# Wider weight blocks and equal token groups in the HGRN2 mixer of a two-layer diffusion backbone

## The chip, the cores and the metric

The kernel runs on one core of a Trainium2 chip. Its metric is the device time of one execution in microseconds (us); the median of three runs before the change is 1749.47 us, from 1747.55 to 1752.41. Names of engines in the profile: PE is TensorE's matrix product, PEld its loading of the stationary operand, DVE is VectorE, ACT is ScalarE, POOL is GpSimd, SP is SyncE, which here issues the large loads.

## The reference

Two layers on 768 tokens of width 1024: 512 latent tokens and a prefix of 256 context tokens, which reads only itself. Each layer is a mixer and a SwiGLU feed-forward network (FFN, inner width 2816). Each sub-layer has an RMS norm and a modulation (shift, scale) ahead of it, and a norm and a gate behind it. Shift, scale and gate are products of two conditioning vectors with `mod_w` (1024 x 6144 per layer). Layer 0 mixes by gated linear attention and grouped-query attention. Layer 1, where most of the change lies, mixes by HGRN2:

```python
fq, f_fwd, f_bwd, fi, fog = _split(h @ w_in, ODD_SIZES)          # five parts of 1024 columns
q = _heads(jax.nn.silu(fq), HGRN_HEADS)                           # 8 heads of 128
i = _heads(fi, HGRN_HEADS)                                        # the values
og = _heads(fog, HGRN_HEADS)                                      # the gates
for d, f in enumerate((f_fwd, f_bwd)):
    log_f = logaddexp(log(lb[d]), log1p(-lb[d]) + log_sigmoid(f)) # forget gates
    k = -expm1(log_f)
    dirs.append(_directional_scan(q, k, i, log_f, n_ctx, reverse=(d == 1)))
o_lat = _gated_readout(dirs[0][1] + dirs[1][1], og[:, :, n_ctx:], out_norm)   # rms(o) * silu(og)
```

The readout goes through `odd_w_out`, and then the last FFN follows. All is fp32.

## The kernel before

An fp32 product is made of three products of the kind fp32r: each operand is split into a high part (H, rounded) and a rest (L), and `mm3` (line 706) issues high by high, high by low and low by high into one accumulation in PSUM. All matmuls are recorded at line 371 and all transposes by PE at line 374. The contraction over 1024 has 8 k-tiles of 128, so a product of one 128-wide stationary tile has 24 matmuls.

**Weights** come in units of 128 x 1024 elements (512 KB). `unit` (from line 685) loads one on SP into a `raw` buffer (three of them), ACT casts it to the high part `wH` (line 699), and DVE subtracts it for the low part `wL` (line 700); there are four pairs `wH`/`wL`. `nat_units` cuts half the k-tiles of a block of columns into units: one of 4 k-tiles by 256 columns, or two of 2 k-tiles by 512.

**Two forms of product.** `gemm_T` keeps the weights stationary and moves tokens, in groups of up to 512 columns of a PSUM tile of two banks with 512 columns each; its result has features on the partitions. It makes the queries, the forget gates (`ff`, two directions for 8 heads, 768 tokens each, so 16 products) and the queries and keys of the first mixer (`gqk`, four products). `gemm_nat` keeps a tile of 128 tokens stationary and moves the weights; its result has tokens on the partitions (`nat`). It makes the values (6 token tiles, as three pairs) and the gates (4 latent tiles, as two pairs), in blocks of 256 columns.

**The order in time around the change.** (1) Near the end of FFN 0, `values()` in `run` makes the first 512 columns of the values, in pieces between the norms of token tiles that come out of the FFN; some units go to tiles that the FFN no longer uses (`go`, `uo`, `macc`). These are the rows `nat<-oH`, `nat<-ogo` and the like. (2) `odd_mixer` makes the other 512 columns, and a generator `late` beside it loads 24 pieces of `mod_w` (tiles `mraw`, three buffers, on SP at line 477), which DVE sums (lines 552 and 554, `macc`). PE adds the sums across partitions (`mod_acc`), DVE copies them (`modrows`, line 485), and PE transposes them (`modT`). (3) For 8 heads, `prep` makes forget gates and queries and `head` scans; pieces of three heads are interleaved by hand with `go`, each call of which advances generators to their next `yield`. (4) Behind the last head come the `gate` blocks, between the last scans: a Silu on ACT (line 1443, into a tile of the tag `mraw` with two buffers) and a product on DVE with the readout. (5) `gated_T` transposes the gated readout (`catT`, ACT copies it at line 1270 and DVE makes its low part), and `out_proj` multiplies by `odd_w_out` (`oproj`), whose units pass through the same `raw` buffers.

Each engine works through its own queue in order, and so does each DMA queue. The queues' order is settled when the program is built. While `self.pinned` is set (heads and gates), PE keeps the order in which the code issues its work; the weight casts and splits on ACT and DVE may come to stand elsewhere than where the code has them.

Of the kernel before, what the change touches and what calls it, by code (L numbers as in the profile page):

```python
# [17 lines left out]
P = 128  # L18
# [321 lines left out]
class Net:  # L340
# [384 lines left out]
    def nat_units(self, w, c0, n, half, to=None):  # L725
        src = w[half * 512 : half * 512 + 512, c0 : c0 + n].rearrange("(k p) m -> p k m", p=P)
        if 4 * n <= WU:
            return [self.unit(src, 4, n, to=to)]
        return [self.unit(src[:, 2 * q : 2 * q + 2, :], 2, n) for q in range(2)]

    def gemm_nat(self, w, c0, n, h, tiles, evac, psum=None, us=None):

        us = us or self.nat_units(w, c0, n, 0) + self.nat_units(w, c0, n, 1)
        kp = KD // len(us)
        for t0 in tiles:
            pt = (psum or self.mm_tile)("nat").rearrange("p (a b) -> p a b", a=2)
# [12 lines left out]

# [308 lines left out]
    def even_mixer(self, h, mix, zu, last):  # L1058
# [7 lines left out]
        groups = ((0, 512), (512, 256))  # L1066
# [56 lines left out]
        def qk(c):  # L1123
            Ws = {x: self.unit_cols(w, x * P) for x in (c, c + 2)}
            yield
            for x in (c, c + 2):
                pt = self.mm_tile(f"gqk{x}")
                for g in groups:
                    self.gemm_T(pt, Ws[x], h, (g,))
                    if g is groups[-1]:  # L1130
                        t = gqk[x // 2] if c == 0 else mixg.tile([P, NT], F32, tag=f"gqk{x // 2}", bufs=1, name=f"gqk{x}")
                        if x < 2:
                            nc.scalar.mul(t, pt[:, :NT], 0.125)
                            gq[c] = t
                        else:
                            nc.scalar.copy(t, pt[:, :NT])
                            gk[c] = t
                    yield
# [186 lines left out]
    def odd_values(self, fi, h, c0, tiles, us=None):  # L1325


        def ev(t0, pt):
            self.nc.scalar.copy(fi[:, t0 : t0 + 2, c0 : c0 + 256], pt[:, :, :256])  # L1329

        self.gemm_nat(self.I["odd_w_in"][0], 3 * D + c0, 256, h, tiles, ev, us=us)

    def odd_mixer(self, h, fi):
# [14 lines left out]
        with self.pool("hg") as gp:  # L1348
            ones = gp.tile([P, CTX], F32, tag="ones", name="ones")
            nc.gpsimd.memset(ones, 1.0)  # L1350
            def prep(hd, given):
# [5 lines left out]
                for d in range(2):  # L1357
                    pt = self.mm_tile(f"ff{hd}{d}")
                    W = self.unit_cols(w, (1 + d) * D + hd * P)
                    self.gemm_T(pt, W, h, ((512, 256),))  # L1360
                    yield
                    self.gemm_T(pt, W, h, ((0, 512),))
                    sg = gp.tile([P, NT], F32, tag="sg", bufs=2, name="sg")
                    nc.scalar.activation(sg, pt[:, :NT], AF.Sigmoid)
# [73 lines left out]
            def gate(c0):  # L1438
                us = self.nat_units(w, 4 * D + c0, 256, 0) + self.nat_units(w, 4 * D + c0, 256, 1)

                def eo(t0, pt):
                    s = self.wp.tile([P, WU], F32, tag="mraw", bufs=2, name="silu")[:, :512].rearrange("p (a n) -> p a n", a=2)
                    nc.scalar.activation(s, pt[:, :, :256], AF.Silu)
                    o = fi[:, t0 : t0 + 2, c0 : c0 + 256]
# [24 lines left out]
            g = [gate(c0) for c0 in (0, 256, 512, 768)]  # L1469
            go(scan, g[0])  # L1470
            go(outs, old)
            go(g[0])
            go(outs, old, scan)
            go(g[1], g[1])
            go(scan, scan)
            go(g[2])
            go(scan)
            go(g[2])
            go(scan)
            go(g[3], g[3])  # L1480
# [152 lines left out]
    def run(self):  # L1633
# [132 lines left out]
        def ending(ys):  # L1766
            ep = self.open_pool("e0b")

            def values():

                to = [[fp.tile([P, D], F32R, tag=x, bufs=1, name=f"o{x}") for x in ("go", "uo")]]
# [3 lines left out]
                self.odd_values(ys, h1, 0, (4,), us)  # L1775
                yield
                self.odd_values(ys, h1, 0, (0,), us)
                yield
                us2 = [u for half in range(2) for u in self.nat_units(I["odd_w_in"][0], 3 * D + 256, 256, half)]
                self.odd_values(ys, h1, 256, (4,), us2)  # L1780
                yield
                self.odd_values(ys, h1, 0, (2,), us)
                self.odd_values(ys, h1, 256, (0, 2), us2)
# [80 lines left out]
```

## Time and profile before

| What | Time |
|---|---|
| median of three runs | 1749.47 us (1747.55 to 1752.41) |
| the profiled execution | 1749.34 us |
| its span (first to last instruction) | 1747.5 us, so 1.84 us lie around it |
| mean granted clock of TensorE | 0.993 of full speed |
| ending of FFN 0 with the first values | 930 to 980 us of the span |
| second half of the values | 980 to 1027 us |
| heads, with the forget gates | 1027 to 1267 us |
| gates, and start of the output projection | 1267 to 1350 us |

A row of the timeline has the start in the span, the duration, engine and line, output and operands, form and number of instructions, and, in brackets, how long the engine idled before and what released it. Durations of matmuls overlap, since they are pipelined: the distance of two starts is what a matmul takes. "nat<-wH,x" is a product of the high weights with a token tile x; `wL` is the low part. SPq is SP's DMA queue. A row of groups has the number of instructions, their busy time and mean in ns, and the idle time before them with its main releaser.

### The profile page before, as it was taken

The numbers are of one execution on the slowest core, as the hardware profiler recorded it, in microseconds if no ns is written. First come the engines' busy times: TensorE is split into PE (matmuls) and PEld (weight loads), VectorE is DVE, ScalarE is ACT, GpSimd is POOL, SyncE is SP. The second block draws the span as 40 slices with busy tenths as digits, with TensorE's granted clock in tenths as the row PEclk, the third lists the DMA queues.
The fourth block names the chain that finished last, engine by engine and source line by source line (L and its number), as shares of the span: only waits on it lengthen the run. The fifth ranks groups of instructions, "written<-read, shape, count | busy, mean of one in ns | idle before, by whom it ended". The sixth has DMA issues, their size and how long they took to land. (4 is left out here: it accounts for less than half of the span.)

```text
span 1747.5 us, 32790 instructions
## 1 busy us (share of the span) xinstructions
PE 1700.9 (97%) x13732; PEld 1526.0 (87%) x13732; DVE 1280.9 (73%) x2036; ACT 857.8 (49%) x1473; POOL 74.2 (4%) x93
## 2 busy tenths in 40 slices
PE   6999999999999999999999999999999999999998
PEld 4889986788999989989998988889898899989997
DVE  5879658735966979787668658787764678878785
ACT  5545557746543333333347336666644664344342
POOL 1004100001000000000001000000000100000000
PEclk8999999999999999999999999999999999999999
DMA  8731013154322424332234752121114333233333
GB/s 318 222 112 39 3 39 107 36 156 139 113 90 73 153 77 156 109 110 61 73 123 143 262 160 63 48 62 50 50 62 133 121 98 108 86 102 106 99 106 120
DMA packets 169647, 187.23 MB, mean 107 GB/s; under 512 B 6262, under 2 KB 140956, under 8 KB 169500
## 3 DMA queue, kind: packets, MB, share of 16 engines
q1 hardware_dynamic: 167568, 181.56, 32.8%
q10 hardware_dynamic: 1932, 3.59, 0.7%
q8 instruction: 107, 1.75, 0.4%
q14 instruction: 40, 0.33, 0.1%
HBM read 175.66 MB, written 9.46 MB: 106 GB/s over the span
## 5 line engine op out<-in xcount | busy, mean ns | idle before, releaser
L371 PE MATMUL nat<-wH,x 128*128 128x256 f32 (+1 forms) x1216 | 229.0, 287 | 0.4 <-issue 0.4
L754 ACT CAST wH<-raw 128x1024 fp32r<-128x1024 f32 x120 | 124.5, 1051 | 197.2 <-PE acc L371 86.2
L700 DVE TENSOR_TENSOR wL<-raw,wH 128x1024 fp32r<-128x1024 f32 (+1 forms) x126 | 151.3, 1206 | 84.3 <-ACT wH L699 83.9
L371 PEld LDWEIGHTS nat<-wH,x 128*128 128x128 f32 x1216 | 193.3, 193 | 3.8 <-ACT y L1329 0.8
L755 DVE TENSOR_TENSOR wL<-raw,wH 128x1024 fp32r<-128x1024 f32 x120 | 145.2, 1221 | 64.9 <-ACT wH L754 64.8
L699 ACT CAST wH<-raw 128x1024 fp32r<-128x1024 f32 (+1 forms) x126 | 128.9, 1038 | 127.8 <-PE nat L371 34.4
L371 PE MATMUL nat<-wL,x 128*128 128x256 f32 (+1 forms) x608 | 173.4, 285 | 0.0
L371 PE MATMUL acc<-wH,gH 128*128 128x512 f32 x440 | 171.8, 390 | 0.0
L371 PE MATMUL acc<-wH,gL 128*128 128x512 f32 x440 | 171.5, 390 | 0.0
L371 PE MATMUL acc<-wL,gH 128*128 128x512 f32 x440 | 171.5, 390 | 0.0
L847 DVE TENSOR_TENSOR y<-y,acc 128x1024 f32<-128x1024 f32 x135 | 115.2, 863 | 37.0 <-PE acc L371 32.8
L554 DVE SCALAR_TENSOR_TENSOR macc<-mraw,scT,macc 128x1024 f32<-128x1024 f32 x98 | 122.6, 1277 | 10.7 <-DMA mraw<-in_mod_w_dram 10.4
L371 PE MATMUL ff<-x,wH 128*128 128x512 f32 (+1 forms) x512 | 127.6, 340 | 0.0
L624 POOL TENSOR_TENSOR rs<-ms,neghalf 128x1 f32<-128x1 f32 (+2 forms) x62 | 58.0, 937 | 1543.2 <-DVE ms L622 1543.1
L371 PEld LDWEIGHTS nat<-wL,x 128*128 128x128 f32 x608 | 117.3, 193 | 0.0
L371 PE MATMUL oproj<-wH,x 128*128 128x512 f32 x320 | 102.5, 397 | 3.2 <-ACT x L1270 3.2
L371 PEld LDWEIGHTS acc<-wH,gL 128*128 128x128 f32 x440 | 82.6, 188 | 17.3
L371 PEld LDWEIGHTS acc<-wH,gH 128*128 128x128 f32 x440 | 82.7, 188 | 16.6
L371 PEld LDWEIGHTS acc<-wL,gH 128*128 128x128 f32 x440 | 82.7, 188 | 16.5
L371 PEld LDWEIGHTS ff<-x,wH 128*128 128x128 f32 x512 | 87.3, 190 | 10.1
L955 ACT COPY qkh<-arr 128x512 f32<-128x512 f32 x112 | 70.1, 642 | 36.3 <-DVE arr L960 32.1
L371 PE MATMUL ff<-x,wL 128*128 128x256 f32 (+1 forms) x256 | 86.2, 337 | 0.0
(344 smaller groups left out, 4047.2 us busy)
## 6 DMA issues: line engine op xcount, KB each, us to landing
mraw<-in_mod_w_dram SPq DMA_DIRECT2D x96, 512.0 KB, 4.8
raw<-in_ffn_w_gate_dram SPq DMA_DIRECT2D x44, 512.0 KB, 3.7
raw<-in_ffn_w_up_dram SPq DMA_DIRECT2D x44, 512.0 KB, 3.8
raw<-in_ffn_w_down_dram SPq DMA_DIRECT2D x44, 512.0 KB, 3.6
raw<-in_odd_w_in_dram SPq DMA_DIRECT2D x40, 512.0 KB, 3.7
raw<-in_even_w_in_dram SPq DMA_DIRECT2D x16, 512.0 KB, 4.6
x<-xr SPq DMA_DIRECT2D x14, 512.0 KB, 2.6
xr<-x SPq DMA_DIRECT2D x14, 512.0 KB, 8.1
```

The source lines that it names most:

```text
L371: return self.pin(self.nc.tensor.matmul(*a, **k))
L554: nc.vector.scalar_tensor_tensor(a, u, w, a, op0=ALU.mult, op1=ALU.add)
L624: nc.gpsimd.tensor_tensor(rs, ms, self.neghalf.to_broadcast([P, w]), op=ALU.pow)
L699: nc.scalar.copy(H[:, :m], raw[:, :m])
L700: nc.vector.tensor_tensor(L[:, :m], raw[:, :m], H[:, :m].bitcast(F32), op=ALU.subtract)
L754: self.nc.scalar.copy(H, f)
L755: self.nc.vector.tensor_tensor(L, f, H.bitcast(F32), op=ALU.subtract)
L847: nc.vector.tensor_tensor(y, y, pt, op=ALU.add)
L955: nc.scalar.copy(qkv[:, :, :, half, :], dst)
```

## The change

It has three parts.

First, the values and the gates are made in blocks of 512 columns, each of four units of 2 k-tiles by 512, in place of blocks of 256 with two units of 4 k-tiles. In the second half of the values there is one block, with ten steps of `late` behind each of three pairs of token tiles, where there were two blocks with five. The gates are two blocks, each in four pieces of one token tile, where there were four blocks of two pieces; the product of a gate with the readout is put off to a list that `gated()` works off, and the calls of `go` stand in another order. In the ending of FFN 0 the one block is made in halves of k (`nat_part`): tokens 4 and 5 with the first half, then tiles 0 and 1, then the second halves, and so on; the first half's units lie in the FFN's old tiles, the second half's in `wH` and `wL`.

Second, products over 768 tokens go as two groups of 384, each in a bank of its own, in place of 512 and 256: the 16 `ff` products of the heads and the four `gqk` products of the first mixer. The offset given to `gemm_T` puts tokens 384 to 767 at column 512 of the PSUM tile, and ACT reads the result as 2 x 384.

Third, as a consequence, 7655 rows stand in PE's list where 8135 stood: 480 matmuls fewer. The number of loads is the same.

```diff
-        return [self.unit(src[:, 2 * q : 2 * q + 2, :], 2, n) for q in range(2)]
+        return [self.unit(src[:, 2 * q : 2 * q + 2, :], 2, n, to=to and to[q]) for q in range(2)]
...
+    def nat_part(self, pt, us, h, t, half):
+
+        kp = 4 // len(us)
+        for k in range(4):
+            W = us[k // kp]
+            self.mm3(
+                pt, h.hl(4 * half + k, slice(t * P, t * P + P)), (W[0][:, k % kp, :], W[1][:, k % kp, :]),
+                half == 0 and k == 0, half == 1 and k == 3,
+            )
...
-        groups = ((0, 512), (512, 256))
+        groups = ((0, 384, 0), (384, 384, -128))
...
-                    self.gemm_T(pt, Ws[x], h, (g,))
+                    self.gemm_T(pt, Ws[x], h, (g[:2],), g[2])
...
-        for c0 in range(512, D, 256):
-            us = self.nat_units(w, 3 * D + c0, 256, 0) + self.nat_units(w, 3 * D + c0, 256, 1)
-            for t0 in (4, 0, 2):
-                self.odd_values(fi, h, c0, (t0,), us)
-                for _ in range(5):
-                    next(late, None)
+        us = [u for half in range(2) for u in self.nat_units(w, 3 * D + 512, 512, half)]
+        for t0 in (4, 0, 2):
+            self.gemm_nat(w, 3 * D + 512, 512, h, (t0,), lambda t, pt: nc.scalar.copy(fi[:, t : t + 2, 512:D], pt), us=us)
+            for _ in range(10):
+                next(late, None)
...
-                    self.gemm_T(pt, W, h, ((512, 256),))
+                    self.gemm_T(pt, W, h, ((384, 384),), -128)
                     yield
-                    self.gemm_T(pt, W, h, ((0, 512),))
+                    self.gemm_T(pt, W, h, ((0, 384),))
...
-                us = self.nat_units(w, 4 * D + c0, 256, 0) + self.nat_units(w, 4 * D + c0, 256, 1)
...
-                for t0 in (0, 2):
-                    self.gemm_nat(w, 4 * D + c0, 256, h, (t0,), eo, us=us)
-                    yield
+                us = [u for half in range(2) for u in self.nat_units(w, 4 * D + c0, 512, half)]
+                for t in range(LT):
+                    pt = self.mm_tile("nat")[:, :512]
+                    for half in range(2):
+                        self.nat_part(pt, us[2 * half : 2 * half + 2], h, t, half)
+                    s = self.wp.tile([P, WU], F32, tag="mraw", bufs=2, name="silu")[:, :512]
+                    nc.scalar.activation(s, pt, AF.Silu)
+                    o = fi[:, t, c0 : c0 + 512]
+                    todo.append((o, s))
+                    yield
...
-            g = [gate(c0) for c0 in (0, 256, 512, 768)]
+            g = [gate(c0) for c0 in (0, 512)]
...
-                us = [u for half in range(2) for u in self.nat_units(I["odd_w_in"][0], 3 * D, 256, half, to[half])]
+                us = [self.nat_units(w, 3 * D, 512, 0, to)]
...
+                part(4, 0)
                 yield
+                us.append(self.nat_units(w, 3 * D, 512, 1))
+                part(0, 0)
                 yield
+                part(4, 1)
                 yield
+                part(0, 1)
+                part(2, 0)
+                part(2, 1)
```

The pieces move instructions on two engines whose queues PE waits for. The first place is DVE's queue where the values end and the heads begin. `macc` are the sums of `mod_w`, `gt` is a copy of gate columns, `L700` the weight splits, `modrows` the copy that PE waits for, `pr` the first work of a head. Before:

```order
L554 SCALAR_TENSOR_TENSOR macc_10238<-mraw_10304,scT,macc_10238 128x1024
L497 TENSOR_TENSOR modcol_10001<-modT,col 128x8
L497 TENSOR_TENSOR modcol_10002<-modT,col 128x8
L600 TENSOR_TENSOR gc_10229<-modcol_10001,col 128x8
L554 SCALAR_TENSOR_TENSOR macc_10238<-mraw_10357,scT,macc_10238 128x1024
L606 COPY gt_10233<-gcT_10231 8x128
L700 TENSOR_TENSOR wL<-raw,wH 128x1024 x2
L485 COPY modrows<-mod_acc 128x512
L1375 MEMSET pr 128x1
```

Now:

```order
L497 TENSOR_TENSOR modcol_9863<-modT,col 128x8
L497 TENSOR_TENSOR modcol_9864<-modT,col 128x8
L600 TENSOR_TENSOR gc_9979<-modcol_9863,col 128x8
L554 SCALAR_TENSOR_TENSOR macc_9988<-mraw_10051,scT,macc_9988 128x1024
L606 COPY gt_9983<-gcT_9981 8x128
L554 SCALAR_TENSOR_TENSOR macc_9988<-mraw_10054,scT,macc_9988 128x1024
L554 SCALAR_TENSOR_TENSOR macc_9988<-mraw_10057,scT,macc_9988 128x1024
L700 TENSOR_TENSOR wL<-raw,wH 128x1024 x3
L485 COPY modrows<-mod_acc 128x512
L1378 MEMSET pr 128x1
```

Two more of the sums stand behind the `gt` copy, and three weight splits, not two, ahead of `modrows`.

The second place is ACT's queue at the end of the gates: the last two Silus, the casts of `odd_w_out` (line 699), and the first copies of `catT`. Before:

```order
L615 DMA gv_14268<-gd_10235 128x1024
L1509 ACT_TABLE_LOAD
L699 CAST wH<-raw 128x1024
L1443 ACTIVATE silu<-nat 128x512
L699 CAST wH<-raw 128x1024 x2
L1443 ACTIVATE silu<-nat 128x512
L1270 ACTIVATE x_14194<-catT,col 128x512 x2
```

Now (lines 1443 and 1270 have become 1448 and 1281):

```order
L615 DMA gv_13776<-gd_9985 128x1024
L1524 ACT_TABLE_LOAD
L1448 ACTIVATE silu<-nat 128x512
L699 CAST wH<-raw 128x1024 x3
L1448 ACTIVATE silu<-nat 128x512
L1281 ACTIVATE x_13702<-catT,col 128x512 x2
L699 CAST wH<-raw 128x1024
```

The next to last Silu has moved ahead of the casts, and all three casts stand between the two Silus.

More of the change, by code (lines that the diff above doesn't have):

```diff
@@ L1128, in qk @@
                 for g in groups:
-                    self.gemm_T(pt, Ws[x], h, (g,))
+                    self.gemm_T(pt, Ws[x], h, (g[:2],), g[2])
                     if g is groups[-1]:
                         t = gqk[x // 2] if c == 0 else mixg.tile([P, NT], F32, tag=f"gqk{x // 2}", bufs=1, name=f"gqk{x}")
+                        pv, tv = (v.rearrange("p (b n) -> p b n", b=2)[:, :, :384] for v in (pt, t))
                         if x < 2:
-                            nc.scalar.mul(t, pt[:, :NT], 0.125)
+                            nc.scalar.mul(tv, pv, 0.125)
                             gq[c] = t
                         else:
-                            nc.scalar.copy(t, pt[:, :NT])
+                            nc.scalar.copy(tv, pv)
                             gk[c] = t
@@ L1322, in att_prep @@
                 nc.gpsimd.tensor_tensor(x, x, rs[:, hs][:, :, None].to_broadcast([P, n, 64]), op=ALU.mult)
[L1325 to L1331, printed above, removed]
     def odd_mixer(self, h, fi):
@@ L1359, in prep @@
                     W = self.unit_cols(w, (1 + d) * D + hd * P)
-                    self.gemm_T(pt, W, h, ((512, 256),))
+                    self.gemm_T(pt, W, h, ((384, 384),), -128)
                     yield
-                    self.gemm_T(pt, W, h, ((0, 512),))
+                    self.gemm_T(pt, W, h, ((0, 384),))
                     sg = gp.tile([P, NT], F32, tag="sg", bufs=2, name="sg")
-                    nc.scalar.activation(sg, pt[:, :NT], AF.Sigmoid)
+                    pv, sv = (v.rearrange("p (b n) -> p b n", b=2)[:, :, :384] for v in (pt, sg))
+                    nc.scalar.activation(sv, pv, AF.Sigmoid)
                     lb, lb1, nlb1 = (x[:, d, hd : hd + 1] for x in (self.lb, self.lb1, self.nlb1))
@@ L1438, in gate, with gated @@
             def gate(c0):
-                us = self.nat_units(w, 4 * D + c0, 256, 0) + self.nat_units(w, 4 * D + c0, 256, 1)
[L1441 to L1444, printed above, removed]
+                us = [u for half in range(2) for u in self.nat_units(w, 4 * D + c0, 512, half)]
[8 more added lines that the diff above has]
+                    yield
+            todo = []
+            def gated():
+                while todo:
+                    o, s = todo.pop(0)
                     nc.vector.tensor_tensor(o, o, s, op=ALU.mult)
-                for t0 in (0, 2):
-                    self.gemm_nat(w, 4 * D + c0, 256, h, (t0,), eo, us=us)
-                    yield
             def go(*xs):
@@ L1468, in odd_mixer @@
                 outs, old, scan = scan, new, head(hd, *given[0])
-            g = [gate(c0) for c0 in (0, 256, 512, 768)]
+            g = [gate(c0) for c0 in (0, 512)]
             go(scan, g[0])
+            gated()
             go(outs, old)
             go(g[0])
+            gated()
             go(outs, old, scan)
-            go(g[1], g[1])
+            go(g[0])
+            gated()
+            go(g[0])
+            gated()
             go(scan, scan)
-            go(g[2])
+            go(g[1])
             go(scan)
-            go(g[2])
+            go(g[1])
             go(scan)
-            go(g[3], g[3])
+            gated()
+            for _ in range(2):
+                go(g[1])
+                gated()
             self.pinned = False
@@ L1769, in values, with part @@
             def values():
+                w = I["odd_w_in"][0]
                 to = [[fp.tile([P, D], F32R, tag=x, bufs=1, name=f"o{x}") for x in ("go", "uo")]]
                 to.append([fp.tile([P, D], F32R, tag="macc", bufs=2, name=f"o{x}") for x in "HL"])
-                us = [u for half in range(2) for u in self.nat_units(I["odd_w_in"][0], 3 * D, 256, half, to[half])]
+                us = [self.nat_units(w, 3 * D, 512, 0, to)]
+                pts = {}
+                def part(t0, half):
+                    if half == 0:
+                        pts[t0] = self.mm_tile("nat").rearrange("p (a b) -> p a b", a=2)
+                    for a in range(2):
+                        self.nat_part(pts[t0][:, a, :], us[half], h1, t0 + a, half)
+                    if half:
+                        nc.scalar.copy(ys[:, t0 : t0 + 2, 0:512], pts.pop(t0))
                 yield
-                self.odd_values(ys, h1, 0, (4,), us)
+                part(4, 0)
                 yield
-                self.odd_values(ys, h1, 0, (0,), us)
+                us.append(self.nat_units(w, 3 * D, 512, 1))
+                part(0, 0)
                 yield
-                us2 = [u for half in range(2) for u in self.nat_units(I["odd_w_in"][0], 3 * D + 256, 256, half)]
-                self.odd_values(ys, h1, 256, (4,), us2)
+                part(4, 1)
                 yield
-                self.odd_values(ys, h1, 0, (2,), us)
-                self.odd_values(ys, h1, 256, (0, 2), us2)
+                part(0, 1)
+                part(2, 0)
+                part(2, 1)
                 ep.release()
```

## The prediction, made before the changed kernel ran

> **What bounds the kernel now.** The page was read first, then the busy times by stretch for the four places the change touches, then the timeline of single instructions inside them.
>
> ```profile
> span 1747.5 us, 32790 instructions
> PE 1700.9 (97%) x13732; PEld 1526.0 (87%) x13732; DVE 1280.9 (73%) x2036; ACT 857.8 (49%) x1473; POOL 74.2 (4%) x93
> ```
>
> PE is busy for 97% of the span, but that share is a mean over the stages, so the places must be looked at singly. The stretches below are, in order: the ending of the first FFN with the first half of the values (930 to 980), the second half of the values (to 1027), the heads with the ff gates (to 1267), the gates and the start of the output projection (to 1350). The columns are the length, busy time and instruction count of PE, its weight loads, DVE, ACT and POOL, the granted clock, the DMA share and GB/s.
>
> ```profile
> 930.00:980.00 50.00, 47.41 (x326) 42.88 (x325) 35.21 (x49) 38.57 (x85) 6.12 (x9) 1.00 0.52 178
> 980.00:1027.00 47.00, 46.13 (x382) 43.95 (x380) 31.26 (x30) 9.95 (x14) 0.32 (x1) 1.00 0.77 257
> 1027.00:1267.00 240.00, 239.19 (x2875) 212.10 (x2872) 181.99 (x397) 145.51 (x246) 8.46 (x6) 1.00 0.19 56
> 1267.00:1350.00 83.00, 79.39 (x796) 75.19 (x795) 47.37 (x86) 38.52 (x59) 2.02 (x2) 0.98 0.32 103
> ```
>
> PE idles 2.6, 0.9, 0.8 and 3.6 us in them, with the clock at full in all but the last (0.98). So here a product removed shortens the span, as long as weights and operands keep up. No other engine is above 77% (DVE in the third). The question is then what a product costs by its width. A duration of one matmul (0.40 us for two, 0.28 for one) overlaps its neighbour's, so the starts must be used, first and last of a steady run for each width:
>
> ```profile
> 1267.92 0.40 PE L371 MATMUL nat<-wH,x 128*128 128x256 f32 x2
> ...
> 1272.24 0.40 PE L371 MATMUL nat<-wH,x 128*128 128x256 f32 x2
> ```
>
> Between these starts stand 12 triples of 256 columns (each k-tile is one row of two and one of one): 4.32/36 = 0.1200 us each. The output projection has the same roles, tokens stationary and weights moving, at 512 columns:
>
> ```profile
> 1344.11 0.62 PE L371 MATMUL oproj<-wH,x 128*128 128x512 f32 x2
> ...
> 1352.27 0.62 PE L371 MATMUL oproj<-wH,x 128*128 128x512 f32 x2
> ```
>
> 12 triples in 8.16 us: 0.2267 us each. For 384 columns, with both kinds of stationary operand, the first mixer has a run:
>
> ```profile
> 564.61 0.51 PE L371 MATMUL E<-x,wH 128*128 128x384 f32 x2
> ...
> 567.73 0.51 PE L371 MATMUL ab<-x,dH 128*128 128x384 f32 x2
> ```
>
> 6 triples in 3.12 us: 0.1733 us. The three points lie on one line: 53.3 ns more for every 128 columns, and 13.3 ns that each matmul pays whatever its width (120.0 − 106.7).
>
> **The change part by part.**
>
> *Blocks of 512.* 960 matmuls of 256 columns become 480 of 512. Values: 4 blocks x 6 token tiles x 8 k x 3 = 576, now 288; gates: 4 x 4 x 8 x 3 = 384, now 192. Each pair costs 0.2400 now and 0.2267 then, 13.3 ns less. Where the 512-wide rows are slowest, at 1241.15 to 1241.85, three take 0.70 us, 0.2333 each, which leaves 6.7 ns a pair:
>
> ```profile
> 1241.15 0.62 PE L371 MATMUL ff<-x,wH 128*128 128x512 f32 x2
> ...
> 1241.85 0.62 PE L371 MATMUL ff<-x,wH 128*128 128x512 f32 x2
> ```
>
> That run follows small work; the long runs have 0.2267 without exception, so I take 13.3. Ending of FFN 0: 144 pairs, 1.92 us; second half of the values: 144 pairs, 1.92; gates: 192 pairs, 2.56. Together 6.4 us, at the lower bound 3.2.
>
> The Trainium skill ("TensorE: Matmul & The Clock Gate", section "Back-to-back issue gap") gives the gap of one isolated matmul as N/2.4 + 2.5 ns, so a part of 2.5 ns that does not grow with the width, where the rows have 13.3. By it the sum of the widening would be 480 x 2.5 = 1.2 us; the trace disagrees, and the sum goes by the trace.
>
> *Groups of 384.* 512 + 256 becomes 384 + 384, as many matmuls and as many columns. On the ff products the pair is in the rows:
>
> ```profile
> 1242.53 0.62 PE L371 MATMUL ff<-x,wH 128*128 128x512 f32 x2
> ...
> 1245.25 0.62 PE L371 MATMUL ff<-x,wH 128*128 128x512 f32 x2
> ...
> 1246.28 0.40 PE L371 MATMUL ff<-x,wH 128*128 128x256 f32 x2
> ...
> 1248.44 0.40 PE L371 MATMUL ff<-x,wH 128*128 128x256 f32 x2
> ```
>
> 0.680 per k at 512 and 0.360 at 256 (2.72/4 and 2.16/6), together 1.040, against 2 x 0.520 for two of 384: nothing, in the ff gates and in the first mixer alike. The first half of a head's ff product now also takes tokens that the later chain does not wait for alone (48 matmuls of 0.1733 either way); ACT's activation reads two banks in place of one piece, same 768 columns. I count 0, with ±1 us for the 20 places (16 ff products, four of the first mixer).
>
> *Weight units.* The 40 loads and splits stay 40, each with as many bytes; what changes is that a block needs four units before it ends, where two sufficed.
>
> ```profile
> raw<-in_odd_w_in_dram SPq DMA_DIRECT2D x40, 512.0 KB, 3.7
> L699 ACT CAST wH<-raw 128x1024 fp32r<-128x1024 f32 (+1 forms) x126 | 128.9, 1038 | 127.8 <-PE nat L371 34.4
> L700 DVE TENSOR_TENSOR wL<-raw,wH 128x1024 fp32r<-128x1024 f32 (+1 forms) x126 | 151.3, 1206 | 84.3 <-ACT wH L699 83.9
> ```
>
> A unit is ready 3.7 + 1.04 + 1.21 ≈ 6 us after its load starts. The split buffers are four and the raw ones three. In a block's last token tile the first buffer comes free when 18 of 24 matmuls are still ahead: 18 x 0.227 = 4.1 us before the end. Three raw units then lie loaded, so cast and split of the next first unit fit (2.25 us); only its fourth, whose load can start when the first raw is released, is 6 us away, and PE needs it 4.1 us + the scan pieces between + three units of 6 matmuls (4.1 us) later. I count 0 here. If that cover is gone, it is the rival (c) below.
>
> *Ending of FFN 0.* ACT's cast before the first late token tile already waited for a load:
>
> ```profile
> 964.97 1.05 ACT L699 CAST wH<-raw 128x1024 fp32r<-128x1024 f32 x1 [4.36 <-DMA raw<-in_odd_w_in_dram]
> ```
>
> Behind it in ACT's queue stand the hf scalings of the next token tile, which PE's products need. With products that are shorter by 1.9 us, I let 0.5 us of it be lost to this wait: −1.4, between 0 (the load sets the end) and −1.9.
>
> *From the values to the heads.* The second half of the values runs beside the modulation sums (24 loads of 512 KB) and ends at a row of sums that goes through DVE and back to PE. DVE's and PE's rows:
>
> ```profile
> 967.72 44.97 SPq L477 DMA_DIRECT2D mraw<-in_mod_w_dram  x24
> 1018.57 1.29 DVE L554 SCALAR_TENSOR_TENSOR macc<-mraw,scT,macc 128x1024 f32<-128x1024 f32 x1 [1.45 <-DMA mraw<-in_mod_w_dram]
> 1025.89 1.23 DVE L700 TENSOR_TENSOR wL<-raw,wH 128x1024 fp32r<-128x1024 f32 x1 [3.37 <-ACT wH L699]
> 1027.23 0.69 DVE L485 COPY modrows<-mod_acc 128x512 f32<-128x512 f32 x1
> 1026.09 1.06 PE L371 MATMUL mod_acc<-macc,one 128*32 128x512 f32 x8
> 1027.97 0.66 PE L374 MATMUL modT<-ident,modrows 128*128 128x128 f32 x4 [0.81 <-DVE pr L1375]
> 1028.38 0.48 PE L371 MATMUL ff<-x,wH 128*128 128x256 f32 x2
> ```
>
> The sums end at 1019.9 and PE comes to them at 1026.1: 6.2 us of slack, of which the shorter products (1.4 + 1.9) take about 3.3. So the ring of loads doesn't become the bound. On DVE three weight splits, not two, stand ahead of the modrows copy; three times 1.22 after 1019.9 is 1023.6, and PE arrives at about 1022.8 and would find modrows ready at 1024.5 at the latest, with the 0.8 us idle of today grown by up to 1. I count the whole −1.9 and let the 1 us be in the range. At worst the gain of this part and of the one before is eaten here.
>
> *End of the gates.* Here a stall goes. PE, then ACT:
>
> ```profile
> 1327.43 1.04 PE L374 MATMUL catT<-ident,y 128*128 128x128 f32 x8
> 1331.67 0.50 PE L371 MATMUL oproj<-wH,x 128*128 128x512 f32 x1 [3.21 <-ACT x L1270]
> 1326.19 1.05 ACT L699 CAST wH<-raw 128x1024 fp32r<-128x1024 f32 x1 [0.94 <-PE nat L371]
> 1329.50 1.04 ACT L699 CAST wH<-raw 128x1024 fp32r<-128x1024 f32 x1 [2.26 <-DMA raw<-in_odd_w_out_dram]
> 1330.45 0.59 ACT L1443 ACTIVATE silu<-nat 128x512 f32<-128x512 f32 x1
> 1330.94 1.26 ACT L1270 ACTIVATE x<-catT,col 128x512 fp32r<-128x512 f32 x2
> ```
>
> PE ended the last gate at 1327.4 and transposed; the copies of those transposes (L1270) stood on ACT behind the last Silu, this behind a cast, and this behind a load of the output weights until 1329.50. In the changed order ACT has three casts between the last two Silus, but of weights whose buffers the last gate's own matmuls free 4.1, 2.7 and 1.4 us before its end, and whose loads are by then long issued, since a block of 512 asks for no unit of the gates any more. The last of the three casts then ends 0.3 us before the gate does. What is late next is the copy itself: two copies of 0.63 after the first transposes, about 0.9 us of idle instead of 3.21: −2.3 us, between 0 (the loads come no earlier) and −3.2.
>
> *Sum* against the profiled execution's own 1749.34 us (span 1747.5 and 1.84 around it; the median of the runs, 1749.47, is 0.13 above): −1.4 − 1.9 − 2.56 − 2.3 ± 0, together −8.2: **1741.2 us**, −0.47%.
>
> **The rivals.** Called the same below is a change under 0.3% (5.25 us), about what a measurement of this kernel can tell from none.
>
> (a) *Handed back at the seams.* The products shorten, but the values' part is held by the cast that waits at 964.97 and by the third split ahead of modrows (0 instead of −3.3), and the loads at the end of the gates come as late as today (0 instead of −2.3). For it: both waits stand in the rows with a load as releaser. Against it: 6.2 us of slack at the sums, and the changed order of ACT. Only the gates' −2.56 is left: 1746.8. With one of the two seams lost, 1743.5 to 1744.5.
>
> (b) *A wide matmul is no cheaper per column when its weights have just changed.* Then the pair saves nothing or the 2.5 ns named above beside the page: 1745.8 to 1747.0 with the tail's −2.3. Against it stand all three widths on one line, the 512 one with the very roles of the changed products.
>
> (c) *Slower: the four buffers have no room for a prefetch.* A block of four units fills all split buffers, so the next block's fourth unit isn't started before the first is released. If a release comes later than its raw buffer's turn, a whole load, cast and split (6 us) is in the open at each of the three block boundaries (values to values, values to gates, gate to gate): 18 − 8.2 = +9.8, 1759. It decides when the first buffer comes free less than 2.25 us before the block's end; I reckon 4.1. For it: the 127.8 us in which ACT's casts already wait, mostly for PE to free a buffer. Against it: the scans between the pieces, and heads between values and gates.
>
> (d) *More than reckoned.* The full 3.2 us at the tail, the 0.5 us of the ending and up to 1 us from the 384 groups also come: 1738.
>
> **How the numbers follow.** Forecast (all terms within about 2 us of the sum, 1739 to 1743.5): 0.62. (a): 0.18, of it a third under 1744.1, the rest the same. (b): 0.05, the same. (c): 0.06 with its milder forms (one boundary, 1747 to 1753). (d): 0.09. Faster: 0.62 + 0.09 + 0.06 = 0.77. Same: 0.12 + 0.05 + 0.02 from (c) = 0.19. Slower: 0.04. The range reaches from a little under (d), 1737.0, to a little over (a), 1747.0; it leaves out the far end of (d) and nearly all of (c), about 0.12.
>
> **What would show each step.** Right: the wide nat rows start 0.227 us apart, and PE has 480 matmuls fewer (13732 to about 13250); the ff products take 0.520 per k and group; ff starts at about 1025 and not 1028.4; the last Silu follows its gate at once, and the idle time of the first oproj row falls from 3.21 to about 0.9. Wrong: rows of 0.24 at 512; modT or nat with an idle time over 2 us behind DVE modrows or ACT's casts; nat rows that wait for a split at block boundaries; a silu that still stands behind a cast with a load as releaser.

## The result, and the profile after

The changed kernel takes 1739.67 us in the median (1738.56 to 1742.42), the kernel before, in four executions beside it, 1748.59 (1747.55 to 1752.41). The ratio is 0.9947, with a 95% interval of 0.9928 to 0.9967: 8.9 us or 0.5% faster. The forecast was 1741.2. The profiled execution took 1738.56 us, with a span of 1736.4; it is the fastest of its four.

The first lines of the page after, then the four stretches of the change (columns as in the prediction: length, then busy time of PE, PEld, DVE, ACT, POOL, the clock, the DMA share, GB/s):

```profile
span 1736.4 us, 31825 instructions
PE 1691.2 (97%) x13252; PEld 1516.2 (87%) x13252; DVE 1280.1 (74%) x2036; ACT 857.3 (49%) x1467; POOL 75.7 (4%) x93
```

```profile
928.80:976.50 47.70, 46.38 (x222) 37.88 (x222) 35.03 (x49) 38.36 (x82) 6.97 (x9) 1.00 0.53 187
976.50:1019.60 43.10, 42.46 (x196) 33.11 (x194) 32.17 (x31) 9.24 (x9) 0.32 (x1) 1.00 0.80 268
1019.60:1259.00 239.40, 239.23 (x2872) 227.57 (x2873) 180.69 (x396) 145.16 (x246) 8.46 (x6) 1.00 0.20 57
1259.00:1341.00 82.00, 81.26 (x628) 68.03 (x627) 48.70 (x87) 39.94 (x61) 2.15 (x3) 1.00 0.34 106
```

PE has 480 matmuls fewer, and its idle time in the four stretches is 1.3, 0.6, 0.2 and 0.7 us, where it was 2.6, 0.9, 0.8 and 3.6. The rates, from PE's timeline after, first and last start of a run of products of 512 columns, and of one of 384:

```profile
978.33 0.62 PE L371 MATMUL nat<-wH,x 128*128 128x512 f32 x2
...
986.49 0.62 PE L371 MATMUL nat<-wH,x 128*128 128x512 f32 x2
```

```profile
1030.15 0.51 PE L371 MATMUL ff<-x,wH 128*128 128x384 f32 x2
...
1031.71 0.51 PE L371 MATMUL ff<-x,wH 128*128 128x384 f32 x2
```

12 triples in 8.16 us are 0.2267 us a matmul, and 3 triples in 1.56 us are 0.1733: both to the digit what the rows of before gave for other products of those widths. The seam between the values and the heads, on DVE and PE:

```profile
1017.77 1.23 DVE L700 TENSOR_TENSOR wL<-raw,wH 128x1024 fp32r<-128x1024 f32 x1 [0.18 <-ACT wH L699]
1019.02 0.69 DVE L485 COPY modrows<-mod_acc 128x512 f32<-128x512 f32 x1
1017.89 1.06 PE L371 MATMUL mod_acc<-macc,one 128*32 128x512 f32 x8
1019.77 0.66 PE L374 MATMUL modT<-ident,modrows 128*128 128x128 f32 x4 [0.81 <-DVE pr L1378]
1020.18 0.60 PE L371 MATMUL ff<-x,wH 128*128 128x384 f32 x2
```

The third split ends just as PE's sums do, and the wait before modT is 0.81 us, as it was; ff starts at 1020.2, not 1028.4. Two waits further ahead, which the prediction did not look at, stood in the profile of before and are gone (hT are transposes of a normed token tile, and this modT is the first of the two):

```profile
969.88 0.65 PE L374 MATMUL hT<-ident,xn 128*128 128x128 f32 x4 [1.01 <-ACT hf L655]
1015.70 0.66 PE L374 MATMUL modT<-ident,modrows 128*128 128x128 f32 x4 [0.86 <-DVE modrows L485]
```

The end of the gates, on ACT and on PE:

```profile
1312.50 1.06 ACT L699 CAST wH<-raw 128x1024 fp32r<-128x1024 f32 x1 [0.71 <-PE nat L371]
1313.86 1.06 ACT L699 CAST wH<-raw 128x1024 fp32r<-128x1024 f32 x1 [0.30 <-PE nat L371]
1315.22 1.06 ACT L699 CAST wH<-raw 128x1024 fp32r<-128x1024 f32 x1 [0.30 <-PE nat L371]
1316.64 0.60 ACT L1448 ACTIVATE silu<-nat 128x512 f32<-128x512 f32 x1 [0.36 <-PE nat L371]
1317.13 1.26 ACT L1281 ACTIVATE x<-catT,col 128x512 fp32r<-128x512 f32 x2
1316.39 1.04 PE L374 MATMUL catT<-ident,y 128*128 128x128 f32 x8
1317.87 0.50 PE L371 MATMUL oproj<-wH,x 128*128 128x512 f32 x1 [0.44 <-ACT x L1281]
```

The three casts of output weights now wait for nat, that is for buffers that the last gate frees, and no longer for loads. The last Silu follows its gate at once, and the 3.21 us of idle time before the output projection are 0.44.

### The profile page after: what moved, and what is told of

Its sections match the earlier page's. It is cut to its first block, busy times and chain, and to the rows that moved or that the text cites. A ratio compares the mean times of both kernels' runs of the same rounds, so it can differ in the third digit from the quotient of the medians.

```text
span 1736.4 us, 31825 instructions
## 1 busy us (share of the span) xinstructions
PE 1691.2 (97%) x13252; PEld 1516.2 (87%) x13252; DVE 1280.1 (74%) x2036; ACT 857.3 (49%) x1467; POOL 75.7 (4%) x93
## 5 line engine op out<-in xcount | busy, mean ns | idle before, releaser
L764 ACT CAST wH<-raw 128x1024 fp32r<-128x1024 f32 x120 | 124.8, 1052 | 197.7 <-DVE y L857 78.4
L371 PE MATMUL nat<-wH,x 128*128 128x256 f32 (+2 forms) x944 | 214.7, 319 | 0.0
L700 DVE TENSOR_TENSOR wL<-raw,wH 128x1024 fp32r<-128x1024 f32 (+1 forms) x126 | 151.3, 1207 | 59.4 <-ACT wH L699 58.3
L371 PEld LDWEIGHTS nat<-wH,x 128*128 128x128 f32 x944 | 158.2, 191 | 13.6 <-issue 0.8
L371 PE MATMUL nat<-wL,x 128*128 128x256 f32 (+2 forms) x472 | 149.0, 316 | 0.0
L371 PE MATMUL ff<-x,wH 128*128 128x384 f32 x512 | 132.1, 339 | 0.0
L554 DVE SCALAR_TENSOR_TENSOR macc<-mraw,scT,macc 128x1024 f32<-128x1024 f32 x98 | 122.9, 1281 | 7.5 <-DMA mraw<-in_mod_w_dram 7.3
L371 PEld LDWEIGHTS nat<-wL,x 128*128 128x128 f32 x472 | 90.3, 191 | 5.0
L371 PEld LDWEIGHTS ff<-x,wH 128*128 128x128 f32 x512 | 91.3, 188 | 0.4
L371 PE MATMUL ff<-x,wL 128*128 128x384 f32 x256 | 85.6, 335 | 0.0
```

Source lines behind the costliest of these rows:

```text
L371: return self.pin(self.nc.tensor.matmul(*a, **k))
L554: nc.vector.scalar_tensor_tensor(a, u, w, a, op0=ALU.mult, op1=ALU.add)
L700: nc.vector.tensor_tensor(L[:, :m], raw[:, :m], H[:, :m].bitcast(F32), op=ALU.subtract)
L764: self.nc.scalar.copy(H, f)
```

## Where the time went, stage by stage

The first row is the start of the first value product in the span, in us. Each number below it is the distance of two starts in PE's timeline: from there to the first ff, to the first gate, to the first catT of the gated readout, to the first oproj, to the first hT of the last FFN, and at last to the end of PE's last matmul (some 8 us of the span lie behind that). The experiments that the columns name are told in the next section.

| Stage | before | before again | changed | changed again | narrow products | changed, own raw | before, own raw |
|---|---|---|---|---|---|---|---|
| ahead of the values | 950.1 | 950.0 | 948.8 | 948.7 | 949.6 | 949.9 | 951.3 |
| values | 78.25 | 76.98 | 71.41 | 71.85 | 75.10 | 71.46 | 77.69 |
| heads, ff | 238.87 | 238.86 | 239.04 | 239.06 | 239.09 | 239.01 | 238.86 |
| gates | 60.18 | 59.93 | 57.17 | 57.17 | 59.51 | 57.14 | 60.18 |
| to the first oproj | 4.24 | 3.44 | 1.48 | 1.47 | 1.47 | 1.48 | 3.88 |
| output projection | 37.15 | 37.08 | 36.61 | 36.86 | 35.82 | 36.33 | 36.07 |
| last FFN | 370.78 | 371.52 | 374.02 | 374.66 | 370.19 | 368.01 | 366.83 |

From the mean of the first two columns to that of the next two, the stages from the values to the output projection gain 11.4 us (6.0 + 2.9 + 2.4 + 0.4, less 0.2 in the heads), 1.3 are gained ahead of the values, and the last FFN, whose code is the same, gives 3.2 back. The 1.3 us have no cause that a run shows: in six profiles, of the changed kernel and of variants of it, the first row lies anywhere from 948.1 to 949.9.

The wait ahead of the output projection costs more than its idle time. In the two profiles of before and in that of the values alone PE idles 3.21, 2.41 and 2.19 us there, and over the 4 us that follow the granted clock is 0.57, 0.58 and 0.63; in the first of them this makes the 0.98 that the prediction read over its whole last stretch. With 0.44 us of idle, in the changed kernel, it is 1.00; but it is also 1.00 behind 2.8 us of idle in the kernel before with own raw buffers. By an estimate from these shares (4 us x 0.43) up to 1.7 us are lost so. Of that only 0.4 shows as a gain of the stage, where the changed kernel has 0.3 and 0.7 us of PE idle that the kernel before has not.

## The experiments

**The 384 groups alone undone.** The 20 products of 768 tokens are put back to 512 and 256 columns, and with them the copies that read their results; the rest is the changed kernel.

```diff
-        groups = ((0, 384, 0), (384, 384, -128))
+        groups = ((0, 512), (512, 256))
...
-                    self.gemm_T(pt, W, h, ((384, 384),), -128)
+                    self.gemm_T(pt, W, h, ((512, 256),))
...
-                    self.gemm_T(pt, W, h, ((0, 384),))
+                    self.gemm_T(pt, W, h, ((0, 512),))
...
```

> The changed kernel with the groups of 768 tokens put back to 512 and 256 columns in all 20 products; blocks of 512 stay. If a product's time is a fixed 13.3 ns plus its columns, as I hold, the ff products still take 1.040 us per k and the heads (240 us) last as long as with 384 and 384 within 0.5 us: 1739.7 +- 1.5. If the equal groups carry part of the gain (rival), this kernel is 1 to 3 us slower than the changed one, and the heads are longer by that.

Measured: 1739.80 us (1736.13 to 1740.25), ratio to the kernel before 0.9940 (0.9925 to 0.9955); the heads last 238.82 us, against 239.04 with 384. The regrouping is worth nothing, as it must be if a product costs its columns and a fixed part, however the columns are shared between two.

**The gates alone.** The kernel before, with `gate`, `gated` and the order of the last scans taken from the change.

```diff
...
-            g = [gate(c0) for c0 in (0, 256, 512, 768)]
+            g = [gate(c0) for c0 in (0, 512)]
...
```

> The kernel before with the gates alone in blocks of 512 (and the order of the last scans that goes with it). My theory: 192 pairs x 13.3 ns = 2.6 us between the last head and the first transposes, and the wait of 3.21 us before the output projection falls to about 0.5, with about 3.3 us between there and the last FFN; the values' part stays as before. Then 1743 to 1745, if the last FFN keeps its length. If the last FFN's pace is set by its loads and takes back what comes before it (rival), its length grows by about 3 us here too, against the 378.7 us of the profile of before, and the time is 1745 to 1747.

Measured: 1744.74 us (1743.40 to 1746.18), ratio 0.9971 (0.9961 to 0.9982). The gates last 57.13 us, and there are 1.48 us to the first oproj: both gains of the end come with the gates. The last FFN lasts 371.6 us, within 0.9 us of both profiles of before and not 3 us longer, so in this profile the last FFN takes nothing of the gain at the gates' end back.

**The values alone.** The kernel before, with `values` and the loop of `odd_mixer` taken from the change.

```diff
...
-        for c0 in range(512, D, 256):
-            us = self.nat_units(w, 3 * D + c0, 256, 0) + self.nat_units(w, 3 * D + c0, 256, 1)
...
+        us = [u for half in range(2) for u in self.nat_units(w, 3 * D + 512, 512, half)]
...
```

> The kernel before with the values alone in blocks of 512, in the ending of the first FFN and in the second mixer. In the changed kernel the stretch from the first value product to the first ff product went from 78.3 to 71.4 us, of which 288 pairs x 13.3 ns explain 3.8. If the other 3 us belong to the blocks of values (my theory), they appear here too: 71 to 72 us in that stretch, 1741 to 1743 in all, with the wait of 3.21 us at the output projection still there. If they come from the other parts of the change, the stretch lasts 74 to 75 us and the time is 1744 to 1746.

Measured: 1744.52 us (1740.89 to 1745.77), ratio 0.9964 (0.9950 to 0.9979). The values last 71.39 us, so the whole gain there belongs to them. The median missed the expected 1741 to 1743; the profiled execution, at 1745.43, has 375.2 us in the last FFN. The gates have 59.51, and the first oproj comes 3.23 us behind the first catT, with 2.19 us of idle.

**Loads in halves.** In the changed kernel each unit of 2 x 512 is loaded as two halves of 256 columns.

```diff
-            nc.sync.dma_start(out=rv[i * n_p : (i + 1) * n_p], in_=x)
+            for q in range(2 if (k, n) == (2, 512) else 1):
+                c = slice(256 * q, 256 * q + 256) if (k, n) == (2, 512) else slice(0, n)
+                nc.sync.dma_start(out=rv[i * n_p : (i + 1) * n_p, :, c], in_=x[:, :, c])
```

> The changed kernel with each load of a unit of 2 x 512 made in two loads of 256 columns, so with rows of 1 KB in place of 2 KB, as before the change; all else is the same, the bytes too. In the ending of the first FFN a cast waited for a load that took 5.3 us from its issue before and 3.7 us after. If the length of the rows does that (my theory), the load takes over 5 us again, the scalings behind the cast come late, and about 1 to 2 us of PE's waiting there return: 1741 to 1743. If the shorter products or the order of the queues did it (rival), the cast's wait stays at about 3.7 us and the time at 1739.7 +- 1.5.

Measured: 1738.74 us (1737.08 to 1740.22), ratio 0.9938 (0.9924 to 0.9953), the values in 71.77 us. On SP's queue the load is issued at 957.57, and ACT's cast starts 3.8 us later:

```profile
957.57 3.26 SPq L700 DMA_DIRECT2D raw<-in_odd_w_in_dram  x6
961.39 1.05 ACT L701 CAST wH<-raw 128x1024 fp32r<-128x1024 f32 x1 [3.80 <-DMA raw<-in_odd_w_in_dram]
```

So the length of the rows is not what made that load faster; that theory fell. The same distance in the other profiles, between SP's issue and the cast, tells why it could not: with the blocks of 256 it is 5.3, 3.8, 6.1 and 4.8 us (before, before again, gates alone, before with own raw), with the blocks of 512 it is 3.7 to 3.9 in seven profiles and 4.7 in one. It is a spread from one execution to the next, wider with the old blocks, and what sets it stays open.

**Narrow products in wide blocks.** The changed kernel, but each 512-wide product of values and gates is two of 256 columns; loads, units, queues and order stay.

```diff
...
-            self.mm3(
-                pt, h.hl(4 * half + k, slice(t * P, t * P + P)), (W[0][:, k % kp, :], W[1][:, k % kp, :]),
-                half == 0 and k == 0, half == 1 and k == 3,
-            )
+            for c in (slice(0, 256), slice(256, 512)):
+                self.mm3(
+                    pt[:, c], h.hl(4 * half + k, slice(t * P, t * P + P)), (W[0][:, k % kp, c], W[1][:, k % kp, c]),
+                    half == 0 and k == 0 and c.start == 0, half == 1 and k == 3 and c.stop == 512,
+                )
```

> The changed kernel with its loads, units of 2 x 512, blocks and queues as they are, but each 512-wide product of values and gates made as two of 256 columns, so 480 matmuls more, as many as before the change. If the narrower count explains 13.3 ns a pair, the first half of the values' stretch grows by 3.8 us (71.4 to 75.2), the gates' by 2.6 (57.2 to 59.7), 6.4 in all: 1746. The waits that went away besides (0.9 us at the scalings of the last late token tile, 1.0 at its transposes, 0.9 at the first modT, 2.8 at the output projection) stay away if they hang on units, loads and order; they come back, and the time is 1748 to 1750, if they hung on the shorter products.

Measured: 1745.80 us (1740.80 to 1747.79), ratio 0.9978 (0.9966 to 0.9989). The values grow from 71.4 to 75.1 us (3.7 for 288 pairs, 12.8 ns each), the gates from 57.2 to 59.5 (2.3 for 192 pairs, 12.2 ns each). The waits stay away. PE's transposes of the last late token tile, ahead of which PE idled 1.01 us in the profile of before, and the first oproj, in this kernel:

```profile
967.70 1.20 PE L374 MATMUL hT<-ident,xn 128*128 128x128 f32 x8
1324.73 0.50 PE L371 MATMUL oproj<-wH,x 128*128 128x512 f32 x1 [0.44 <-ACT x L1284]
```

That splits the gain of the change in two. The wider products are worth 6 us; the units of 2 x 512, requested four at a time, and the queues' order that follows from them are worth another 5 to 6 us (2.4 before the output projection, 2 to 3 in the values, some 0.5 in the gates), at the same count of matmuls. That is the reading of the stages; units and order were not parted from each other. In the medians the wide products are worth 6.1 us and the rest 3.1 (1748.93 against 1745.80). The profiled execution, 1740.80, is the fastest of the ten and 5 us under their median, and its last FFN is the shortest with shared raw buffers, 370.2; where the other nine lose their time no profile shows.

**The first mixer's values in 512 as well.** The one block holds both halves of the values, made where the first half was.

```diff
...
-                nc.scalar.copy(gv[:, t0 : t0 + 2, 256 * c : 256 * c + 256], pt[:, :, :256])
+                nc.scalar.copy(gv[:, t0 : t0 + 2, :], pt)
...
-            return nat(512 + 256 * c, ev_v)
+            return iter(()) if c else nat(512, ev_v, 512)
```

> The changed kernel, and the first mixer's values (2 blocks of 256, 6 token tiles) in one block of 512 as well: 144 pairs x 13.3 ns = 1.9 us less work for PE, if the stage keeps its pace: 1737.8, with the first product of the first output projection about 1.9 us earlier in the span than 343.5 to 344.6. The blocks come three pieces earlier than the order written out by hand has them, and four units hold all buffers while other units of 8 x 128 stand behind them: if that costs a wait of 6 us once (rival), the time is 1742 to 1744.

Measured: 1743.86 us (1741.80 to 1746.88), 4 us slower than the changed kernel though 144 matmuls fewer. The profiled execution, 1746.88, is the slowest of the nine; in it the first product of the first output projection starts at 352.2 us, not 343.5. In PE's timeline the scans of the first mixer now wait for DVE and ACT where pieces of the second values had been between them:

```profile
184.04 1.15 PE L371 MATMUL pbg<-qkg 64*64 64x64 f32 x32 [2.39 <-DVE CTg L950]
186.36 1.97 PE L371 MATMUL pbg<-qkg 64*64 64x64 f32 x32 [1.16 <-DVE CTg L950]
...
190.83 0.48 PE L371 MATMUL pdg<-gvo,kng 128*64 128x128 f32 x2 [1.03 <-ACT kng L1017]
```

These three waits are 4.6 us, and none over 0.7 us stands there in the changed kernel. It is the cover that was taken from the scans, a rival that I had not named; the expected wait for weights isn't among the waits over 0.7 us. The rest of the 8.7 us is for the most part the clock (the third number from the end), from 185 to 200 us in this kernel and then in the changed one:

```profile
185.00:200.00 15.00, 12.81 (x221) 11.56 (x218) 13.63 (x44) 7.46 (x19) 5.45 (x4) 0.54 0.01 3
185.00:200.00 15.00, 15.00 (x201) 14.59 (x200) 10.58 (x28) 9.81 (x18) 0.60 (x1) 1.00 0.01 2
```

15 us at 0.54 lack 6.9 us of full clock, an estimate from this row. All nine executions have a mean granted clock of 0.990 to 0.993, and the five of the changed kernel 0.994 to 0.996, so the others lost clock too. The saved matmuls, 1.9 us by the forecast's 13.3 ns, are outweighed by waits and clock together.

**Both kernels once more**, for the spread of the stages.

> The kernel before once more, for the spread of its stages from one execution to the next. In the profiles so far the last FFN lasted 370.8 us (before), 371.6 (gates alone), 375.2 (values alone), 374.0, 374.9 and 372.7 (the changed kernel and two near it). If that is spread, this one may lie anywhere in 370 to 375; if the kernel before always has the shorter one (a give-back that belongs to the change), it lies within 0.7 us of 370.8.

> The changed kernel once more, for the same purpose: its last FFN lies within 0.7 us of 374.0 if its length belongs to the change, anywhere in 370 to 375 if it is spread. All stages ahead of it, from the first product of the values on, within 0.5 us of the first profile: 71.4 to the first ff product, 239.0 for the heads, 57.2 to the first transposes of the gated readout, 1.5 and 36.6 to the end of the output projection.

Measured: 1747.44 and 1739.84 us. The stages stand in the table. In the values, before again has no wait at the hT transposes, so the 1.0 us of the first profile is one of the things that vary. The last FFN came within 0.8 us of its first length both times: 371.5 and 374.7. By these four the give-back belongs to the change; but the loads in halves (372.7), the first mixer's values (371.4) and the narrow products (370.2) have the wide blocks too and a shorter last FFN, so the spread of this stage, from 370 to 375 us, is at least as large. PE's idle time over the whole stage is 6.3 and 6.8 us in the two profiles of before and 9.0 and 9.6 in the two of the changed kernel, 2.8 us more in the mean: nearly all of the 3.2.

**Raw buffers of its own for the last FFN.** In that stage PE waits for copies of ACT (uo and go), and these stand behind a cast that waits for a load, in ACT's waits from 1390 to 1690 us of the changed kernel (us in total, times, longest):

```profile
ACT wH L764 <- DMA raw<-in_ffn_w_up_dram: 7.6, 9, 1.3
```

and PE's own waits from 1385 to 1680:

```profile
PE ab L371 <- ACT go L828: 5.3, 8, 1.1
PE ab L371 <- ACT uo L828: 1.1, 1, 1.1
PE ab L371 <- DVE uo L836: 0.7, 1, 0.7
```

The first of these rows in the kernel before, in the same stretch (line 828 is 818 there):

```profile
PE ab L371 <- ACT go L818: 3.8, 7, 1.3
```

The gate and up weights shared three raw buffers with the down weights. In the last FFN, where there is room, they get four of their own:

```diff
-            r = self.wp.tile([P, WU], F32, tag="raw", bufs=3, name="raw")
+            r = (pool if deep == 2 else self.wp).tile([P, WU], F32, tag="rawp" if deep == 2 else "raw", bufs=4 if deep == 2 else 3, name="raw")
```

> The changed kernel with four raw buffers of their own for the gate and up weights of the last FFN, which until now share three with the down weights. The last FFN lasted 370.2 to 375.2 us in ten profiles, in step with its idle time of 5.2 to 9.6 us, and nearly all of that idle time is a cast that waits for a load, once in each of nine rounds. If the load comes late because it has to wait for a raw buffer (my theory), it now starts a round earlier, the idle time falls to about 3 us, the stage lasts 367 to 368 us and the time is 1732 to 1735. If SP's queue or the wL and wH buffers hold it back (rival), the stage stays at 372 to 375 and the time at 1739.7 +- 1.5.

> The kernel before with the same four raw buffers in the last FFN. The stages ahead of the last FFN are shorter by 12 to 14 us in the changed kernel's profiles, the time by only 9. If the difference is given back in the last FFN's waits for loads, then without these waits the two kernels with own buffers differ by the whole 12 us, this one at 1744 to 1747; if the give-back has another cause or is spread, they differ by about 9.

Measured: on the changed kernel 1731.61 us (1730.47 to 1732.97), ratio to the kernel before 0.9900 (0.9886 to 0.9913); on the kernel before 1746.15 us (1742.88 to 1748.74), ratio 0.9982 (0.9973 to 0.9991). PE's waits in the same stretch of the changed kernel with own buffers are one row:

```profile
PE ab L371 <- ACT go L828: 0.5, 1, 0.5
```

and no cast of L764 waits for a load there. PE's busy time from 1380 to 1700 us is the first number after the length, in the changed kernel, and then with own buffers:

```profile
1380.00:1700.00 320.00, 312.79 (x2180) 291.54 (x2180) 254.80 (x354) 150.36 (x237) 0.00 (x0) 1.00 0.33 98
```

```profile
1380.00:1700.00 320.00, 319.39 (x2232) 298.97 (x2232) 259.92 (x358) 155.82 (x243) 0.00 (x0) 1.00 0.33 99
```

Its idle time there falls from 7.2 to 0.6 us, and the stage lasts 368.0 us. The time is a little under the 1732 to 1735 that was expected. This kernel is 8 us faster than the changed one and 17 faster than the one before. Its distance to the kernel before with the same buffers is 14.5 us in the medians and 11.5 in the profiled spans (1731.2 against 1742.7; the first is the slowest of its four, the second 1.6 us under its median), where the two kernels without them are 8.9 apart in the medians. Over the whole last FFN PE now idles 2.5 us in the changed kernel and 2.7 in the one before. The 1.2 us by which the stage is still longer, 368.0 against 366.8, lie in PE's busy time, 365.5 against 364.1: from 1376 to 1383 us the granted clock is 0.76 in the changed kernel with own buffers, a loss of up to 1.7 us by an estimate from that share. So without these waits the change brings its 11.5 us or more: the missing 3 us were lost in the last FFN, in waits behind its loads. Why these waits are longer behind the changed kernel than behind the old one is not shown.

## Why the prediction was right, and where it was not

The forecast was −8.2 us against the profiled 1749.34; the medians moved by 8.9, the two profiled executions by 10.8. It was right for the larger part of its reasons, with two errors of opposite sign: the stages ahead of the last FFN gained 12.7 us, not 8.2, and the last FFN gave 3.2 back, where the sum had nothing. That the total came so near is in part luck.

- **What bounds the kernel**: right. PE's time per product set these stretches, and a matmul of 512 columns costs 0.2267 us in its new place too. The term of 6.4 us for the pairs was taken away alone by the narrow products: 6.0 us.
- **384 groups at 0**: right; 1739.80 without them.
- **Weight units at 0**, and rival (c): right that nothing is exposed. No nat product after waits for a split at a block's end; rival (c), +9.8 us, didn't come.
- **Ending of FFN 0, −1.4, and the seam, −1.9**: mis-sized, and the first with the wrong sign in its correction. I let 0.5 us of the products' gain be lost behind the cast at 964.97. The values gained 6.0 us (mean of two) instead of 3.3: 3.7 from the products, 1.5 from waits that became shorter, not longer (2.9 and 2.0 us of PE idle before, 0.8 and 1.1 after), and 0.8 in PE's busy time that no run explains. The first modT waited 0.86 and 1.16 us for modrows in the two profiles of before, and 0 and 0.29 after; the wait at hT of 1.0 us stood in one profile of before and not in the other. I had worked out only the second modT, where the wait stayed at 0.81, as expected.
- **Gates, −2.56**: 2.9. Of this 2.3 are the products.
- **End of the gates, −2.3**: right in mechanism, 2.4 in size (3.84 to 1.48 in the mean of two). The three casts start 3.9, 2.5 and 1.2 us before the first catT, where I had reckoned buffers that come free 4.1, 2.7 and 1.4 before the gate's end. The idle time left is 0.44, not 0.9. What the wait cost in clock, up to 1.7 us, had no term, though the rows of before showed 0.98.
- **Behind the output projection: no term.** That is the step that failed. The sum took it that a gain ahead of the last FFN stays a gain, since its code doesn't change. That stage lasted 3.2 us longer, 2.8 of them in PE's idle time, in waits for copies of ACT that stand behind casts waiting for loads. The profile of before had shown these waits (3.8 us of PE waiting for ACT), and I did not read that stage. With own raw buffers the waits go, and the whole gain is seen; why the change lengthens them stays open.

Of the rivals, (a) had the right idea, a gain handed back, and the wrong place: both seams it named gained. By (b), with no saving for 512 columns, the narrow products would cost nothing; they cost 6 us. By the 2.5 ns that the Trainium skill ("TensorE: Matmul & The Clock Gate", section "Back-to-back issue gap") adds to the columns of an isolated matmul they would cost 1.2 us, an estimate from that figure; this run disagrees with it. Of (d) the ending did come better than reckoned, and the tail about as reckoned in idle time; its own terms (0.9 + 0.5 + 1) give 1738.8 and not 1738.

## What to carry to other kernels

Each matmul pays a fixed part beside its columns, here 13 ns, so that the widest moving operand a bank takes is some 5% cheaper per column than half of it; sharing the same columns differently among the same number of matmuls is worth nothing. Where PE is the bound, read also the stages behind the change: a stage whose queue already waits for loads, a little in every round, can swallow part of a gain ahead of it, and a buffer there may be worth as much as the change itself. Work that is merged into larger blocks is also cover that is taken from somewhere: the same widening in the first mixer cost 4 us because scans had hidden behind the small pieces. And a wait of PE can cost more than its idle time: look at the granted clock of the few microseconds behind it.

## What was not expected of the hardware

Loads of the same 512 KB, issued at the same place of the program by one queue, took from 3.7 to 6.1 us to the cast that waits for them, and this changed from one execution of a kernel to the next (5.3 and 3.8 for the kernel before). Cutting a load into two of half the row length did not slow it (3.8 us). The last FFN, with equal code, lasted 370.2 to 375.2 us in ten profiles with shared raw buffers. PE's waits in it go from 5.2 to 9.6 us, and with own raw buffers the stage lasted 366.8 and 368.0. In the two longest of the ten (the values alone and the 384 groups undone) up to 1.7 us are clock, by estimates from 7 us at 0.76 each.

Behind short waits of PE the granted clock fell to a half for a while, and not every time: 4 us at 0.57 to 0.63 behind 3.21, 2.41 and 2.19 us of idle ahead of the output projection, none behind 2.8; and 15 us at 0.54 with the three waits of the first mixer's values (4.6 us of idle between 181.7 and 190.8 us). What decides it is not shown.
